# One row block of the third gate chunk ahead of each query and each key-value chunk, and probabilities times values one step later

## The chip, the cores and the metric

The kernel runs on one core of a Trainium2 chip. The metric is the time of one execution in microseconds (us) on the device; for a kernel the median of several runs is given. Profiles come from one execution that the hardware profiler recorded. Five engines matter: TensorE (PE; its weight loads are shown as PEld), VectorE (DVE), ScalarE (ACT), GpSimd (POOL) and SyncE (SP), whose queue issues the weight transfers.

## What is computed

The reference is one encoder layer on 256 tokens of width 4096, in float32. Cut to what matters here:

```
h = rms_norm(x, g_mix);  proj = h @ w_in
c_q, c_kv, k_rope, gate_a, q_b, k_b, v_b, gate_b = split(proj)   # 1024, 512, 64, then 5 x 2048
q  = rms_norm(c_q)  @ w_uq      # 16 heads x (128 + 64 rotary)
kv = rms_norm(c_kv) @ w_ukv     # 16 heads x (128 key + 128 value)
y_a = softmax(q k^T) v          # 16 latent heads, each 256 x 256 scores
y_a = rms_norm(y_a) * silu(gate_a)
y_b = dilated attention of q_b, k_b, v_b, normalised, * silu(gate_b)
x = x + concat(y_a, y_b) @ w_out
x = x + (p @ w_ple) * sigmoid(rms_norm(x) @ w_ple_gate)
out = rms_norm(x)
```

## The kernel before

Every float32 product is done as three products of rounded parts: an operand is split in a high part (ScalarE copies it with rounding, L115) and a low part (VectorE subtracts, L116), and `mm` (L130) issues high x high (L133), then L134 and L135 with one low part each. In the trace the names of the outputs tell them apart: `m` are chunk products, `s` scores, `o` probabilities times values, `t` transposes.

The weights pass through TensorE in *steps*, which are laid out by hand in one list. A `Chunk` is a column block of a weight matrix, and one of its steps takes `per` row blocks of 128 rows (two where nothing else is said): a transfer by SyncE into a `raw` tile (four of them), the split into `hi` and `lo` (a ring of three), and products for both token tiles of 128 tokens. In the main loop (L1425), at each step `i`, first the split of step `i + 2` is queued on ScalarE and VectorE, then the products of step `i` on TensorE, and then `advance()` (L240) moves all running tasks by one stage. Each engine's program order is the order in which this Python code issues.

Tasks are generators; each `yield` ends a stage. `advance()` first starts at most one waiting head (not sooner than two steps behind the last one started, and at most five at a time), then moves the `urgent` tasks, then the running heads, the oldest first.

The stage of the latent heads has eight rounds. Round `i` has a step of the third gate chunk `ga2` (512 columns of the gate, 32 row blocks, two a step, in banks m0 and m1), four steps of query chunk `i` (384 columns, 8 row blocks) and two steps of key-value chunk `i` (512 columns, 4 row blocks). The last two share banks m2 and m3. Behind the last query step `done_uq` (L472) begins: ScalarE copies the product to a tile `T5` (L478), GpSimd rotates the rotary part (L212 to L215), ScalarE copies again (L483), TensorE transposes (L488), and ScalarE and VectorE store the result (L492, L493). Behind the last key-value step `done_uk` (L498) takes the keys (L511, VectorE) and the split values (L118, ScalarE; L119, VectorE) out of the banks, one token tile after the other, and puts two heads in the waiting list, which may start once `done_uq` has ended. The first one of such a pair is called head A, the second head B.

A latent head is the generator `attend` (L386) with `dil` false. Its stages, one for each step: transposes of query and key (L393, L394); their split; scores `s` (ten products); maximum and exponentials (L415, L417); reciprocal and scaling (L433, L438); transposes of the probabilities (L443); their split into `pt` (L446); probabilities times values `o` (six products); the copy of `o` to the head's output and its square (L456, L458). Transposes take the banks t0 and t1 in turn; there is one bank each for `s` and `o`.

After the eight rounds the remaining eight steps of `ga2` and sixteen of a fourth gate chunk `ga3` follow, while the last heads end. Then come the projections of the dilated heads, those heads themselves with the last gate chunks, the output projection and the last stage with the embeddings.

Of the kernel before, what the change touches and what calls it, by code (L numbers as in the profile page):

```python
# [66 lines left out]
class Chunk:  # L67
# [1 line left out]

    def __init__(self, src, nk, n, lhs, banks, done, needs=lambda j: (), per=2, ts=(0, 1), keep=None):
        self.src, self.nk, self.n, self.lhs, self.banks = src, nk, n, lhs, banks
        self.done, self.needs, self.per, self.ts, self.keep = done, needs, per, ts, keep
        self.ps = None


@with_exitstack
def encoder_layer(ctx: ExitStack, tc: tile.TileContext, x, p, positions, g_mix, w_in, g_q_latent, w_uq,
# [18 lines left out]
    def bank(tag, shape, bufs=1):  # L98
        names[tag] = names.get(tag, 0) + 1
        return pp.tile([P, *shape], F32, tag=tag, name=f"{tag}_{names[tag]}", bufs=bufs)  # L100
# [8 lines left out]
    def plain(t):  # L109
        return t.bitcast(F32)  # L110

    def split(hi, lo, src, scale=None):

        if scale is None:
            nc.scalar.activation(hi, src, AF.Copy)  # L115
            nc.vector.tensor_tensor(lo, src, plain(hi), op=ALU.subtract)  # L116
        else:
            nc.scalar.activation(hi, src, AF.Copy, scale=scale)  # L118
            nc.vector.scalar_tensor_tensor(lo, src, scale, plain(hi), op0=ALU.mult, op1=ALU.subtract)  # L119
# [266 lines left out]
    def attend(h, q_src, k_src, pe, v, y, dil):  # L386

        tp = turn_bank([4, P])
        for t in range(NT):
            nc.tensor.transpose(tp[:, t], q_src(t), ident)  # L393
            nc.tensor.transpose(tp[:, NT + t], k_src(t), ident)  # L394
        yield
        qk = slot(f"T{h % 2}", [2, 4 * P], F32R)
        split(qk[:, 0], qk[:, 1], tp.rearrange("p a b -> p (a b)"))
        if dil:
            flags.add(("read", h))
        yield  # L400
        s = bank("s", [NT, S])
        for t in range(NT):
            a = tuple(qk[:, i, t * P:(t + 1) * P] for i in range(2))
            b = tuple(qk[:, i, S:] for i in range(2))
            mm(s[:, t], a, b, True, pe is None)
            if pe is not None:
                both = pe[0]()[:, t * P:(t + 1) * P]
                nc.tensor.matmul(s[:, t], both, pe[1][0], start=False, stop=False)
                nc.tensor.matmul(s[:, t], both, pe[1][1], start=False, stop=True)
        yield  # L410
        i = h % 2
        e = E["t"][:, i]
        nmax, l, rl = E["s"][:, i, 0], E["s"][:, i, 1], E["s"][:, i, 2]
        if not dil:
            nc.vector.tensor_reduce(nmax, s, axis=AX.X, op=ALU.max, negate=True)  # L415
            for t in range(NT):
                nc.scalar.activation(e[:, t], s[:, t], AF.Exp, bias=nmax[:, t:t + 1], accum_out=l[:, t:t + 1])  # L417
        else:
            flat = "p a b -> p (a b)"
            nc.vector.scalar_tensor_tensor(e.rearrange(flat), E["d"][:, 0].rearrange(flat), -SLOPES[h],  # L420
                                           s.rearrange(flat), op0=ALU.mult, op1=ALU.add)
            nc.vector.tensor_reduce(nmax, e, axis=AX.X, op=ALU.max, negate=True)
            yield
            for t in range(NT):
                nc.scalar.activation(e[:, t], e[:, t], AF.Exp, bias=nmax[:, t:t + 1])
            yield
            for t in range(NT):
                nc.vector.scalar_tensor_tensor(e[:, t], e[:, t], 1.0, E["d"][:, 1, t], op0=ALU.mult,
                                               op1=ALU.mult, accum_out=l[:, t:t + 1])
            nc.vector.reciprocal(rl, l)  # L430
        yield
        if not dil:
            nc.vector.reciprocal(rl, l)  # L433
        for t in range(NT):
            if dil:
                nc.scalar.activation(e[:, t], e[:, t], AF.Copy, scale=rl[:, t:t + 1])
            else:
                nc.vector.tensor_scalar(e[:, t], e[:, t], rl[:, t:t + 1], None, op0=ALU.mult)  # L438
        yield
        tp = turn_bank([NT, S])  # L440
        for k in range(NT):
            for t in range(NT):
                nc.tensor.transpose(tp[:, k, t * P:(t + 1) * P], e[:, t, k * P:(k + 1) * P], ident)  # L443
        yield
        pt = slot(f"T{2 + h % 2}", [2, NT, S], F32R)
        split(pt[:, 0], pt[:, 1], tp)  # L446
        if dil:
            vs = slot(("Q0", "T6")[h % 2], [2, NT, HD], F32R)
            split(vs[:, 0], vs[:, 1], v)
            v = lambda kt: (vs[:, 0, kt], vs[:, 1, kt])  # L450
        yield
        o = bank("o", [S])
        for k in range(NT):
            mm(o, v(k), tuple(pt[:, i, k] for i in range(2)), k == 0, k == NT - 1)
        yield
        nc.scalar.activation(y, by_token(o) if dil else o, AF.Copy)  # L456
        sq = junk[:, S * i:S * (i + 1)] if h else acc
        nc.scalar.activation(sq, o, AF.Square)  # L458
        if h:
            nc.gpsimd.tensor_tensor(acc, acc, sq, op=ALU.add)  # L460
        flags.add(("head", dil, h))

    def by_token(a):
        return a.rearrange("p (t c) -> p t c", t=NT)
# [7 lines left out]
    def done_uq(i):  # L472
        def task(ps):
            q = slot("T5", [NT, 2, NOPE + ROPE])
            kq = slot("T6", [1024])
            pairs[i] = {"q": q, "kq": kq}
            for t in range(NT):
                nc.scalar.activation(q[:, t].rearrange("p h c -> p (h c)"), ps[t], AF.Copy, scale=rqs[:, t:t + 1])  # L478
            both = kq[:, 512:].rearrange("p (t h d r) -> p t h d r", t=NT, h=2, d=2)
            rotate(both[:, :, :, 0], q[:, :, :, NOPE:], both[:, :, :, 1], 2)  # L480
            yield
            yield
            nc.scalar.activation(both[:, :, :, 1], both[:, :, :, 0], AF.Copy)  # L483
            yield
            tp = turn_bank([2, S])
            for h in range(2):
                for t in range(NT):
                    nc.tensor.transpose(tp[:, h, t * P:(t + 1) * P], both[:, t, h].rearrange("p d r -> p (d r)"),  # L488
                                        ident)
            yield  # L490
            pe = slot("Q0", [2, S], F32R)
            nc.scalar.activation(pe, tp, AF.Copy)  # L492
            nc.vector.tensor_tensor(pe[ROPE:], tp[ROPE:], plain(pe[ROPE:]), op=ALU.subtract)  # L493
            pairs[i]["pe"] = pe
            flags.add(("uq", i))
        return task
# [28 lines left out]
    def lhs_c(key):  # L525
        return lambda kt: (cT[key][0][:, kt], cT[key][1][:, kt])
# [227 lines left out]
    class Step:  # L754
# [4 lines left out]
        def __init__(self, load, split, run, needs=(), frees=0):  # L759
            self.load, self.split, self.run, self.needs, self.frees, self.after = load, split, run, needs, frees, None  # L760
            self.ring = WP
# [363 lines left out]
    M = ("m0", "m1"), ("m2", "m3")  # L1125
# [8 lines left out]
    def add(ch, lo=0, hi=None):  # L1134
        steps.extend((ch, j) for j in range(lo, ch.nk // ch.per if hi is None else hi))

    def cols(w, lo, n):
        return w[:, lo:lo + n]
# [59 lines left out]
    lay(blk, order, gates_mid(blk), gates_done(blk))  # L1198
    ga2 = from_x(OFF_GA + 1024, 512, done_gate(0, 2))
    ga2.banks, other = M  # L1200
    for i in range(8):
        add(ga2, i, i + 1)
        add(Chunk(cols(w_uq, 384 * i, 384), 8, 384, lhs_c("q"), other, done_uq(i), lambda j: ["latents"]))
        add(Chunk(cols(w_ukv, 512 * i, 512), 4, 512, lhs_c("kv"), other, done_uk(i), lambda j: ["latents"]))
    hook(len(steps), lambda: spawn(y_stats(0)))
    hook(len(steps) + 1, lambda: spawn(x_sums()))
# [21 lines left out]
    for c in range(4):  # L1228
        if c == 3:
            hook(len(steps) + 8, lambda: spawn(y_sums()))  # L1230
        ch = from_x(OFF_GB + 512 * c, 512, done_gate(1, c))
# [33 lines left out]
    for c, (lo, n) in enumerate(blocks):  # L1265
        if c < 2 * WIDE:
            continue
        w, per = cols(w_ple_gate, lo, n), 1024 // n
# [20 lines left out]
    class Old(Step):  # L1289
# [40 lines left out]

        def run(self, hi, lo):
            ch, j = self.ch, self.j
            if j == 0:
                ch.ps = [bank(b, [512]) for b in ch.banks]
            for k in range(ch.per):
                kt = ch.per * j + k
                a = ch.lhs(kt)
                for t in ch.ts:
                    mm(ch.ps[t][:, :ch.n], tuple(q[:, t * P:(t + 1) * P] for q in a), (hi[:, k], lo[:, k]),
                       kt == 0, kt == ch.nk - 1)  # L1340
            if ch.per * (j + 1) == ch.nk:
                self.after = lambda: ch.done([q[:, :ch.n] for q in ch.ps])
# [82 lines left out]
    for i, step in enumerate(steps):  # L1425
# [23 lines left out]
        n = 0  # L1449
# [33 lines left out]
```

## Time and profile before

| | |
|---|---|
| median of 3 runs | 1947.0 us (1946.75 to 1947.37) |
| the profiled execution | 1946.98 us, span 1944.7 us |
| mean granted TensorE clock | 0.997 |
| busy share of the span | PE 99%, PEld 84%, DVE 76%, ACT 55%, POOL 4% |
| bytes moved by DMA | 370.57 MB, mean 191 GB/s |
| share of the chain that ended last | PE 96%, DVE 2%, ACT 1% |

The profile's span begins with the first recorded instruction; the execution's own time is 2.3 us longer. Times in the trace are us from the span's start. The latent stage with its eight rounds runs from about 243 us to 433 us. In the timeline a row has the start, the duration, the engine, the line, the operation, output and input names and shapes, and the count; what stands in brackets is how long the engine was idle before it and what it waited for. The durations of products are modelled and overlap, so distances between starts are the better measure. A row of the waits has who waited for whom, the us in total, the times and the longest.

### The profile page before, as it was taken

The page shows a single profiled execution, that of the slowest core. Times are in us where ns is not written, and L with a number is a line of the kernel's source. Part 1 is how long each engine was busy: PE and PEld are TensorE (multiplying, and loading weights), DVE is VectorE, ACT ScalarE, POOL GpSimd, SP SyncE. Part 2 cuts the span into 40 slices and gives each one's busy share as a digit, 9 for nine tenths or more (in the row PEclk, how much of TensorE's full clock was granted, in tenths as well). Part 3 has the DMA queues.
Part 4 walks back from the last instruction along what each step waited for, and adds up shares of the span by engine and source line. Part 5 has one row for each costly group of instructions (what it writes and reads, how often), then busy time and mean ns, then how long its engine had stood idle before and what let it go on. Part 6 is the DMA issues. An engine that isn't in the chain of part 4 may idle for free.

```text
span 1944.7 us, 25491 instructions
## 1 busy us (share of the span) xinstructions
PE 1918.8 (99%) x9317; PEld 1636.6 (84%) x9317; DVE 1487.4 (76%) x2053; ACT 1079.2 (55%) x1478; POOL 81.6 (4%) x124
## 2 busy tenths in 40 slices
PE   9999999999999999999999999999999999999997
PEld 8998888888888888888888888888888888888887
DVE  7767965556888878878677777888866598888765
ACT  6555565555555555545446676555555455655543
POOL 1001012221000000000000100000000000000000
PEclk9999999999999999999999999999999999999999
DMA  7666654445566666566664446665656556566655
GB/s 249 189 184 197 195 168 127 125 138 163 180 209 205 200 201 217 191 199 196 202 210 141 152 143 225 211 213 183 206 188 218 187 189 218 191 222 203 225 185 178
DMA packets 146476, 370.57 MB, mean 191 GB/s; under 512 B 11924, under 2 KB 45808, under 8 KB 146096
## 3 DMA queue, kind: packets, MB, share of 16 engines
q1 hardware_dynamic: 144432, 361.80, 58.2%
q0 software_dynamic: 1920, 7.15, 1.1%
q8 instruction: 73, 1.20, 0.2%
q14 instruction: 51, 0.42, 0.1%
HBM read 364.72 MB, written 4.19 MB: 190 GB/s over the span
## 4 chain that ended last, share of the span: by engine, by line
PE 96%; DVE 2%; ACT 1%; DMA 0%; issue 0%; SPq 0%; DVEq 0%; ACTq 0%
PE m L133 20%; PE m L134 20%; PE m L135 20%; PE t L133 4%; PE t L135 4%; PE t L134 4%; PE o L134 4%; PE o L135 4%; PE o L133 4%; PE s L133 3%; PE s L135 3%; PE s L134 3%; PE t L443 1%; DVE lo L116 1%; ACT hi L115 0%; DMA raw<-in_w_in_dram 0%
## 5 line engine op out<-in xcount | busy, mean ns | idle before, releaser
L116 DVE TENSOR_TENSOR lo<-raw,hi 128x1024 fp32r<-128x1024 f32 (+4 forms) x495 | 552.4, 1127 | 255.9 <-ACT hi L115 254.7
L115 ACT ACTIVATE hi<-raw 128x1024 fp32r<-128x1024 f32 (+4 forms) x495 | 482.4, 982 | 330.0 <-PE m L135 138.4
L133 PE MATMUL m<-hi,Ah 128*128 128x512 f32 (+2 forms) x1118 | 423.8, 379 | 0.0
L134 PE MATMUL m<-lo,Ah 128*128 128x512 f32 (+2 forms) x1118 | 419.0, 375 | 0.7 <-DVE lo L832 0.5
L135 PE MATMUL m<-hi,Al 128*128 128x512 f32 (+2 forms) x1114 | 416.7, 374 | 0.0
L134 PEld LDWEIGHTS m<-lo,Ah 128*128 128x128 f32 x1118 | 210.8, 189 | 31.5 <-DVE lo L116 1.2
L135 PEld LDWEIGHTS m<-hi,Al 128*128 128x128 f32 x1114 | 209.8, 188 | 32.5 <-DVE Al L127 0.2
L133 PEld LDWEIGHTS m<-hi,Ah 128*128 128x128 f32 x1118 | 210.8, 189 | 29.6
L133 PE MATMUL m<-hi,B 128*128 128x512 f32 (+1 forms) x405 | 154.2, 381 | 4.1 <-ACT T L478 3.9
L135 PE MATMUL m<-hi,B 128*128 128x512 f32 (+1 forms) x405 | 150.7, 372 | 0.0
L134 PE MATMUL m<-lo,B 128*128 128x512 f32 (+1 forms) x405 | 150.7, 372 | 0.0
L116 DVE TENSOR_TENSOR B<-raw,B 128x1024 fp32r<-128x1024 f32 (+1 forms) x81 | 87.1, 1088 | 27.7 <-ACT B L115 27.7
L115 ACT ACTIVATE B<-raw 128x1024 fp32r<-128x1024 f32 (+1 forms) x81 | 75.8, 950 | 53.7 <-PE o L135 25.8
L133 PEld LDWEIGHTS m<-hi,B 128*128 128x128 f32 x405 | 76.1, 188 | 16.1 <-ACT T L478 6.1
L135 PEld LDWEIGHTS m<-hi,B 128*128 128x128 f32 x405 | 76.0, 188 | 11.2
L134 PEld LDWEIGHTS m<-lo,B 128*128 128x128 f32 x405 | 76.2, 188 | 10.3 <-DVE lo L116 0.2
L829 ACT ACTIVATE hi<-raw 128x1024 fp32r<-128x1024 f32 x50 | 53.2, 1065 | 54.7 <-PE o L135 22.5
L115 ACT ACTIVATE hi<-B 128x1024 fp32r<-128x1024 f32 x44 | 46.7, 1061 | 41.3 <-PE o L135 28.5
L116 DVE TENSOR_TENSOR T<-t,T 128x512 fp32r<-128x512 f32 (+1 forms) x65 | 43.8, 683 | 32.7 <-ACT T L115 32.5
L133 PE MATMUL m<-B,Ah 128*128 128x512 f32 (+1 forms) x184 | 68.5, 372 | 0.0
L135 PE MATMUL m<-B,Al 128*128 128x512 f32 (+1 forms) x184 | 68.2, 371 | 0.0
L134 PE MATMUL m<-B,Ah 128*128 128x512 f32 (+1 forms) x184 | 68.2, 371 | 0.0
(744 smaller groups left out, 3778.9 us busy)
## 6 DMA issues: line engine op xcount, KB each, us to landing
raw<-in_w_in_dram SPq DMA_DIRECT2D x320, 512.0 KB, 3.9
raw<-in_w_out_dram SPq DMA_DIRECT2D x128, 512.0 KB, 4.6
raw<-in_w_ple_gate_dram SPq DMA_DIRECT2D x128, 512.0 KB, 4.5
raw<-in_w_in_dram SPq DMA_DIRECT2D x63, 400.0 KB, 3.3
raw<-in_w_uq_dram SPq DMA_DIRECT2D x32, 384.0 KB, 3.3
raw<-in_w_ukv_dram SPq DMA_DIRECT2D x16, 512.0 KB, 3.5
T<-in_x_dram SPq DMA_DIRECT2D x7, 512.0 KB, 6.3
T<-in_x_dram POOLq DMA_DIRECT2D x7, 512.0 KB, 7.4
```

Source lines behind the costliest of these rows:

```text
L115: nc.scalar.activation(hi, src, AF.Copy)
L116: nc.vector.tensor_tensor(lo, src, plain(hi), op=ALU.subtract)
L133: nc.tensor.matmul(ps, ah, bh, start=start, stop=False)
L134: nc.tensor.matmul(ps, ah, bl, start=False, stop=False)
L135: nc.tensor.matmul(ps, al, bh, start=False, stop=stop)
L443: nc.tensor.transpose(tp[:, k, t * P:(t + 1) * P], e[:, t, k * P:(k + 1) * P], ident)
L829: nc.scalar.activation(hi, r[1], AF.Copy)
```

## The change

`ga2_1` is a second chunk over the same columns with one row block a step; it stands ahead of each query chunk and of each key-value chunk. The eight steps of two row blocks in the rounds become sixteen of one; the row blocks that are done by the end of the rounds are the same sixteen. The banks are allotted at the first step of `ga2_1` and handed on to `ga2` (`rest`), which does the other sixteen row blocks as before. In `attend`, a latent head has one more `yield` between the split of the probabilities and `o`.

```
-    def __init__(..., per=2, ts=(0, 1), keep=None):
+    def __init__(..., per=2, ts=(0, 1), keep=None, rest=None):
...
-        self.ps = None
+        self.ps, self.rest = None, rest
...
         pt = slot(f"T{2 + h % 2}", [2, NT, S], F32R)
         split(pt[:, 0], pt[:, 1], tp)
+        if not dil:
+            yield
...
     ga2.banks, other = M
+    ga2_1 = Chunk(ga2.src, 32, 512, lhs_x, M[0], None, per=1, rest=ga2)
     for i in range(8):
-        add(ga2, i, i + 1)
+        add(ga2_1, 2 * i, 2 * i + 1)
         add(Chunk(cols(w_uq, 384 * i, 384), 8, 384, lhs_c("q"), other, done_uq(i), lambda j: ["latents"]))
+        add(ga2_1, 2 * i + 1, 2 * i + 2)
         add(Chunk(cols(w_ukv, 512 * i, 512), 4, 512, lhs_c("kv"), other, done_uk(i), lambda j: ["latents"]))
...
         def run(self, hi, lo):
             ch, j = self.ch, self.j
-            if j == 0:
+            if ch.ps is None:
                 ch.ps = [bank(b, [512]) for b in ch.banks]
+                if ch.rest:
+                    ch.rest.ps = ch.ps
```

More of the change, by code (lines that the diff above doesn't have):

```diff
@@ L67, with __init__ @@
 class Chunk:
-    def __init__(self, src, nk, n, lhs, banks, done, needs=lambda j: (), per=2, ts=(0, 1), keep=None):
+    def __init__(self, src, nk, n, lhs, banks, done, needs=lambda j: (), per=2, ts=(0, 1), keep=None, rest=None):
         self.src, self.nk, self.n, self.lhs, self.banks = src, nk, n, lhs, banks
         self.done, self.needs, self.per, self.ts, self.keep = done, needs, per, ts, keep
-        self.ps = None
+        self.ps, self.rest = None, rest
 @with_exitstack
```

## The prediction

> **What bounds the kernel now.** I read the page first, then TensorE's waits, then the timeline of the stage that the diff edits.
>
> ```profile
> PE 1918.8 (99%) x9317; PEld 1636.6 (84%) x9317; DVE 1487.4 (76%) x2053; ACT 1079.2 (55%) x1478; POOL 81.6 (4%) x124
> ```
> ```profile
> PE o L134 <- DVE T L116: 5.5, 7, 0.9
> PE m L133 <- ACT T L478: 3.9, 7, 0.6
> PE t L270 <- DVE lo L116: 1.6, 1, 1.6
> PE m L1416 <- DVE junk L1410: 1.5, 1, 1.5
> PE t L443 <- DVE T L438: 0.3, 1, 0.3
> ```
>
> TensorE is busy all the time, and nothing in the diff changes the number of its products. So only its waits can be won or lost. Outside the start and end the list (us in total, times, longest) has two that repeat, both in the latent stage: the output product `o` waiting for the low half of the probabilities, and the first key-value product waiting for L478, which copies the query chunk out of its bank. A round of that stage takes 24.65 us:
>
> ```profile
> 294.65:319.30 24.65, 23.23 (x138) 21.13 (x137) 14.85 (x24) 13.91 (x30) 6.01 (x9) 1.00 0.42 128
> ```
>
> I call the steps of a round G (two row blocks of the third gate chunk), U0 to U3 (query chunk) and K0, K1 (key-value chunk); heads A and B are the pair whose latents the previous round made. The timeline of TensorE in a round (start, duration):
>
> ```profile
> 288.96 0.28 PE L133 MATMUL o<-T,B 128*128 128x256 f32 x1
> 290.08 0.39 PE L134 MATMUL o<-T,B 128*128 128x256 f32 x1 [0.85 <-DVE T L116]
> ...
> 298.08 0.27 PE L394 MATMUL t<-ident,T 128*128 128x128 f32 x1
> 298.91 0.50 PE L133 MATMUL m<-hi,B 128*128 128x512 f32 x1 [0.56 <-ACT T L478]
> 299.25 0.39 PE L134 MATMUL m<-lo,B 128*128 128x512 f32 x1
> ...
> 304.49 0.28 PE L133 MATMUL s<-T 128*128 128x256 f32 x1
> ...
> 305.68 0.40 PE L133 MATMUL m<-hi,Ah 128*128 128x512 f32 x1
> ...
> 308.44 0.60 PE L488 MATMUL t<-ident,T 128*128 128x128 f32 x4
> 308.87 0.29 PE L443 MATMUL t<-ident,T 128*128 128x128 f32 x1
> ```
>
> From these I take: G's 12 products last 308.44-305.68 = 2.76 us, 0.23 each, so a half G is 1.38; ten score products `s` last 305.68-304.49 = 1.19, 0.12 each; four transposes 0.43, 0.11 each. The first gap is 290.08-288.96-0.12 = 1.00. The second is 298.91-298.08-0.11 = 0.72. After a wait the next product also starts late: 299.25-298.91 = 0.34 instead of 0.23, so 0.11 more. The two waits cost 1.11 and 0.83 us in a full round.
>
> **What the change takes away.** With half a G (g') between U3 and K0, the copy L478 has 1.38 us of products beside it, and head B's transposes no longer stand between U3 and K0 (L478 waits for them now, because they read the tile it overwrites). Taking 0.83 in seven rounds, and 0.43 in the first (rows below: 254.37-254.05 = 0.32, and 0.11), gives 6.2. `o` with another step between loses its wait: six times 1.11, and a seventh idle of 5.5-6x0.85 = 0.4, with the same 0.26 on top 0.66, gives 7.3. With the 0.3 of L443 the gain is 13.8 us at most.
>
> **What it adds.** I wrote down which stage of which head falls behind which step. A round becomes g, U0 to U3, g', K0, K1. The query task finishes one step earlier, so head A starts behind U0 and B behind U2, each with ten stages. Behind the steps TensorE then does: g: B's probability transposes (L443); U0: `o` of A; U2: `o` of B, `s` of the next A, transposes of the next B; g': `s` of the next B; K0: L443 of A; K1: L488. Two places have only half a G of cover, and each comes behind a chain that can begin only when the step before it ends.
>
> *Scores of B, behind g'.* ScalarE works in program order. Behind U3 it has the two L478 copies, the two copies of the last B's output, A's two exponentials, then the high half of B's query-key split; VectorE follows with the low half. How soon L478 comes after U3 shows best in the first round:
>
> ```profile
> 253.36 0.33 PE L135 MATMUL m<-hi,B 128*128 128x384 f32 x1
> ...
> 253.88 0.34 PE L135 MATMUL m<-hi,B 128*128 128x384 f32 x1
> 254.37 0.50 PE L133 MATMUL m<-hi,B 128*128 128x512 f32 x1
> ```
> ```profile
> 253.74 1.11 ACT L478 ACTIVATE T<-m,st 128x384 f32<-128x384 f32 x2 [0.66 <-PE m L135]
> 254.74 1.05 ACT L115 ACTIVATE hi<-raw 128x1024 fp32r<-128x1024 f32 x1
> ...
> 290.98 0.38 ACT L456 ACTIVATE B<-o 128x256 f32<-128x256 f32 x1 [0.72 <-PE o L135]
> ...
> 291.53 1.10 ACT L115 ACTIVATE T<-t 128x512 fp32r<-128x512 f32 x2
> ...
> 302.17 0.48 ACT L417 ACTIVATE T<-s,st 128x256 f32<-128x256 f32 x1 [1.34 <-DVE st L415]
> ...
> 303.09 0.60 ACT L115 ACTIVATE T<-t 128x512 fp32r<-128x512 f32 x1
> ```
> ```profile
> 303.72 0.69 DVE L116 TENSOR_TENSOR T<-t,T 128x512 fp32r<-128x512 f32 x1 [1.58 <-ACT T L115]
> ```
>
> U3's last product starts at 253.88; three products earlier is 253.36, so each takes 0.17 and U3 ends at 254.05. L478 begins 0.05 after the first token tile is done (253.36+0.33), and ScalarE is free at 254.74, 0.69 after U3. The two output copies take 291.53-290.98 = 0.55, the exponentials 303.09-302.17 = 0.92, from high half to low half is 0.63, the low half 0.69, the signal 0.05: 3.53 us after U3. TensorE gets there after g' and one product that needs only the high half: 1.38+0.12 = 1.50. The wait is 2.03, with the restart 2.14; the first such round has no output copies, 1.59. Seven rounds: 6x2.14+1.59 = 14.4 us.
>
> *Probability transposes of B, behind the next g.* Behind K1, VectorE and ScalarE unload the key-value chunk (L511, L118, L119 for each token tile), then split A's probabilities, then VectorE scales B's probabilities, which L443 transposes.
>
> ```profile
> 259.47 0.48 DVE L511 TENSOR_SCALAR T<-m,st 128x256 f32<-128x256 f32 x1 [0.20 <-PE m L135]
> ...
> 289.34 0.69 DVE L116 TENSOR_TENSOR T<-t,T 128x512 fp32r<-128x512 f32 x1
> 289.94 0.16 DVE L433 RECIPROCAL st<-st 128x2 f32<-128x2 f32 x1
> ...
> 305.33 0.48 DVE L511 TENSOR_SCALAR T<-m,st 128x256 f32<-128x256 f32 x1
> ...
> 308.17 0.15 DVE L433 RECIPROCAL st<-st 128x2 f32<-128x2 f32 x1
> 308.36 0.61 DVE L438 TENSOR_SCALAR T<-T,st 128x256 f32<-128x256 f32 x2
> ```
> ```profile
> 259.94 0.39 PE L133 MATMUL m<-hi,Ah 128*128 128x512 f32 x1
> ```
> ```profile
> 307.63 0.83 ACT L115 ACTIVATE hi<-raw 128x768 fp32r<-128x768 f32 x1
> ```
>
> L511 can start 0.47 before K1 is through (259.47 against 259.94). From it to ScalarE's next work is 307.63-305.33 = 2.30, to the low half of A's split 0.63 more, 2.93; VectorE itself is free at 308.17-305.33 = 2.84, so 2.93 holds. The low half takes 289.94-289.34 = 0.60, the reciprocal 0.19, and L443 followed the scaling's start by 308.87-308.36 = 0.51: 4.23, or 3.76 after K1's end. TensorE arrives after L488 and half a G: 0.43+1.38 = 1.81. Now it arrives after the scores, a whole G and L488, 1.19+2.76+0.43 = 4.38, and there is no split before the scaling: that is why L443 waits only 0.3 in all. The new wait is 1.95; six rounds 11.7, and in the last, where a whole G follows, 3.76-0.43-2.76 = 0.57. Together 12.3 us. While L443 waits, U0's bank comes free (VectorE has gone on 2.84 us after L511), so it costs nothing more.
>
> *Small things.* Two more changes a round between transposes and products cost between nothing and the 0.11 of a restart each, 0 to 1.5 us in seven rounds; I take 1.2, near the upper end, since a late product is what every switch in these rows shows. The gate block's split becomes two of 128x512 (0.60 and 0.69 against 1.05 for the large one on ScalarE): about 0.15 us more on each engine, twice a round, under TensorE's products. `o` one step later and one step earlier a start finish the last head behind the same step, so the following stages keep their place. Eight more transfers pass SP's queue:
>
> ```profile
> SPq L1306 <- DVE lo L116: 591.9, 239, 7.9
> ```
>
> SP waits for buffers to be emptied, not the splits for data, so smaller transfers cost nothing; if every one of eight were late by its landing time, that would be the third rival. [...]
>
> The sum: 14.4+12.3+1.2-13.8 = +14.1 us. The profiled execution took 1946.98 us (span 1944.7), the median of the runs is 1947.0. So 1961.0 us.
>
> **Rivals.** *Both covers hold* (faster): if what I queue behind L478 and L511 were done before them, the gains stay and the two new waits do not come: 1947.0-13.8 = 1933.2. Against it: ScalarE sat idle 0.66 before L478 in the row above with work behind it. Chance 0.08. *One of the two new waits does not come*: only the first, 14.4+1.2-13.8 = +1.8; only the second, -0.3. Both are no change that a measurement tells. Chance 0.04. *Transfers late*: the half blocks land 3.9 us after issue as the large ones do, 8x3.9 = +31 over the forecast, 1992:
>
> ```profile
> raw<-in_w_in_dram SPq DMA_DIRECT2D x320, 512.0 KB, 3.9
> ```
>
> Chance 0.02. *Clock*: the granted clock is 1.00 in the round quoted, with gaps of 1 us. If gaps of 2 us lowered it to half for as long as one G, each of 13 waits would cost 2.76 more, 36 us, 1997. Chance 0.02, since no gap reaches it. [...] My forecast has the remaining 0.84.
>
> **How the numbers follow.** Low bound of the forecast: no cost for switching (-1.2), and A's split not ahead of the scaling (-0.6 six times): 1956; some more overlap that I missed, three us, 1953. High: if L478 and L511 could not start on the first token tile while the second is computed, the chains are some 0.5 us longer in 7 places and 0.7 in 6: +7.7, 1969. The range is 1953 to 1970. A measurement of this kernel tells about 0.2%, 3.9 us, from no change; slower takes the forecast, the transfers and the clock, 0.88; same 0.04; faster 0.08.
>
> **What would show it.** In the changed profile the waits of K0 on L478 and of `o` on L116 are gone; instead `s` waits for T (L115, L116) about seven times by 2 us in all its pieces, and L443 for the scaling (by 2 us, six times); a round takes about 26.7 to 27.3 us. Wrong if a round is under 24.65, if either wait is absent, or if waits stand in the stages behind.

## The result and the profile after

The changed kernel takes 1969.28 us (median of 4 runs, 1968.84 to 1969.7) against 1947.04 us; the ratio is 1.0114, 95% interval 1.0097 to 1.0132. It is 22.2 us slower. The forecast was 14.1 us slower, 1961.0 us, with a range from 1953 to 1970. TensorE's busy line of the page and its granted clock in 40 slices:

```profile
PE 1928.8 (98%) x9317; PEld 1641.3 (83%) x9317; DVE 1491.1 (76%) x2061; ACT 1080.4 (55%) x1486; POOL 68.4 (3%) x124
PEclk9999999899999999999999999999999999999999
```

TensorE has the same 9317 products, but it is busy for 1928.8 us instead of 1918.8: some of them became slower. One slice, in the latent stage, has a clock of 8 tenths. TensorE's three longest waits (us in total, times, longest; lines are one to three higher than before, by the lines that the change adds):

```profile
PE t L444 <- DVE T L439: 11.3, 7, 1.8
PE s L134 <- ACT T L116: 8.0, 7, 1.2
PE s L135 <- DVE T L117: 2.4, 7, 0.3
```

The two old waits are gone, and the two forecast ones are there, seven times each. Five rounds of the stage, from one L444 to the next (start and end, length, busy times, granted clock, DMA share, GB/s):

```profile
286.79:315.26 28.47, 25.09 (x136) 22.16 (x137) 15.40 (x26) 14.24 (x31) 3.41 (x8) 0.94 0.35 111
315.26:342.15 26.89, 23.51 (x136) 20.95 (x137) 15.37 (x26) 14.12 (x31) 4.30 (x9) 1.00 0.42 118
342.15:370.60 28.45, 25.07 (x137) 22.32 (x137) 15.38 (x26) 14.24 (x31) 4.29 (x9) 0.94 0.37 111
370.60:400.63 30.03, 26.64 (x137) 23.74 (x137) 15.38 (x26) 14.36 (x31) 4.13 (x9) 0.89 0.38 105
400.63:427.52 26.89, 23.51 (x136) 20.95 (x137) 15.37 (x26) 14.12 (x31) 4.29 (x9) 1.00 0.38 119
```

Where the clock is 1.00, a round takes 26.89 us; the forecast was 24.65 + 2.14 + 1.95 + 0.2 - 1.94 = 27.0. The other rounds are longer by 1.56 to 1.58, or by 3.14, and in these the clock is below 1.00. The timeline of TensorE in the first of them:

```profile
300.38 0.40 PE L136 MATMUL m<-hi,Al 128*128 128x512 f32 x1
302.00 0.39 PE L134 MATMUL s<-T 128*128 128x256 f32 x1 [1.23 <-ACT T L116]
302.73 0.39 PE L135 MATMUL s<-T 128*128 128x256 f32 x1 [0.34 <-DVE T L117]
...
303.42 0.28 PE L135 MATMUL s<-T 128*128 128x256 f32 x1
303.54 0.36 PE L136 MATMUL s<-T 128*128 128x256 f32 x1
...
304.13 0.63 PE L134 MATMUL m<-hi,B 128*128 128x512 f32 x1
304.56 0.63 PE L135 MATMUL m<-lo,B 128*128 128x512 f32 x1
...
306.69 0.55 PE L134 MATMUL m<-hi,B 128*128 128x512 f32 x1
307.08 0.39 PE L135 MATMUL m<-lo,B 128*128 128x512 f32 x1
307.31 0.40 PE L136 MATMUL m<-hi,B 128*128 128x512 f32 x1
...
313.05 0.40 PE L136 MATMUL m<-hi,Al 128*128 128x512 f32 x1
315.26 0.72 PE L444 MATMUL t<-ident,T 128*128 128x128 f32 x4 [1.82 <-DVE T L439]
```

After the half block ends (300.38 + 0.23) TensorE stands still until 302.00 and, but for one product, until 302.73: 2.00 us. Behind that, from 303.6 to 307.0, products start 0.43 us apart instead of 0.23: half clock for 3.4 us (granted clock 0.50). There are five such stretches in this execution, beginning at 303.6, 358.2, 371.9, 388.9 and 443.6, with a granted clock of 0.50 or 0.51 in each. The distances are 54.6, 13.7, 17.1 and 54.6, all whole multiples of 3.41. Five times 1.57 is 7.9 us: with the forecast's 14.1 this is 22.0 of the 22.2 us.

The two chains, on ScalarE and on VectorE, are as forecast:

```profile
298.90 1.10 ACT L481 ACTIVATE T<-m,st 128x384 f32<-128x384 f32 x2 [2.88 <-PE m L136]
299.90 0.38 ACT L459 ACTIVATE B<-o 128x256 f32<-128x256 f32 x1
...
300.43 0.49 ACT L418 ACTIVATE T<-s,st 128x256 f32<-128x256 f32 x1
...
301.32 0.62 ACT L116 ACTIVATE T<-t 128x512 fp32r<-128x512 f32 x1
```
```profile
301.98 0.69 DVE L117 TENSOR_TENSOR T<-t,T 128x512 fp32r<-128x512 f32 x1 [4.09 <-ACT T L116]
...
311.03 0.48 DVE L514 TENSOR_SCALAR T<-m,st 128x256 f32<-128x256 f32 x1 [0.71 <-PE m L136]
...
313.96 0.69 DVE L117 TENSOR_TENSOR T<-t,T 128x512 fp32r<-128x512 f32 x1
...
314.76 0.62 DVE L439 TENSOR_SCALAR T<-T,st 128x256 f32<-128x256 f32 x2
```

ScalarE stood idle 2.88 us before the query chunk's copy (now L481), with the exponentials and the split that TensorE needs queued behind it. VectorE unloads the bank from 311.03, then comes the split (313.96), then the scaling (314.76), and L444 begins 0.50 later.

### The profile page after: what moved, and what is told of

The parts are those of the page before. It is cut to its first block, busy times and chain, and to the rows that moved or that the text cites. A ratio compares the mean times of both kernels' runs of the same rounds, so it can differ in the third digit from the quotient of the medians.

```text
span 1967.1 us, 25558 instructions
## 1 busy us (share of the span) xinstructions
PE 1928.8 (98%) x9317; PEld 1641.3 (83%) x9317; DVE 1491.1 (76%) x2061; ACT 1080.4 (55%) x1486; POOL 68.4 (3%) x124
## 4 chain that ended last, share of the span: by engine, by line
PE 95%; DVE 3%; ACT 1%; issue 0%; DMA 0%; POOL 0%; SPq 0%; DVEq 0%; ACTq 0%; POOLq 0%
PE m L134 20%; PE m L135 20%; PE m L136 20%; PE t L134 4%; PE t L136 4%; PE t L135 4%; PE o L136 4%; PE o L134 4%; PE o L135 4%; PE s L135 3%; PE s L136 3%; PE s L134 3%; PE t L444 1%; DVE T L117 1%; DVE lo L117 0%; DVE B L120 0%
## 5 line engine op out<-in xcount | busy, mean ns | idle before, releaser
L116 ACT ACTIVATE hi<-raw 128x1024 fp32r<-128x1024 f32 (+4 forms) x503 | 480.9, 965 | 360.9 <-PE m L136 160.0
L134 PE MATMUL m<-hi,Ah 128*128 128x512 f32 (+2 forms) x1104 | 418.3, 379 | 0.4 <-ACT Ah L126 0.4
L135 PE MATMUL m<-lo,Ah 128*128 128x512 f32 (+2 forms) x1104 | 413.1, 374 | 0.8 <-DVE lo L835 0.5
L134 PE MATMUL m<-hi,B 128*128 128x512 f32 (+2 forms) x415 | 161.1, 388 | 0.7 <-DVE B L120 0.7
L135 PE MATMUL m<-lo,B 128*128 128x512 f32 (+2 forms) x415 | 156.8, 378 | 0.7 <-DVE lo L117 0.5
L136 PE MATMUL m<-hi,B 128*128 128x512 f32 (+2 forms) x415 | 156.8, 378 | 0.0
L117 DVE TENSOR_TENSOR B<-raw,B 128x1024 fp32r<-128x1024 f32 (+1 forms) x85 | 93.0, 1108 | 27.2 <-ACT B L116 27.0
L116 ACT ACTIVATE B<-raw 128x1024 fp32r<-128x1024 f32 (+1 forms) x85 | 81.0, 966 | 51.3 <-PE o L136 21.7
L134 PEld LDWEIGHTS m<-hi,B 128*128 128x128 f32 x415 | 79.7, 192 | 12.2 <-issue 1.2
L136 PEld LDWEIGHTS m<-hi,B 128*128 128x128 f32 x415 | 79.2, 191 | 12.0
L116 ACT ACTIVATE hi<-B 128x1024 fp32r<-128x1024 f32 x46 | 48.8, 1061 | 47.5 <-PE o L136 30.1
L134 PE MATMUL m<-B,Ah 128*128 128x512 f32 (+1 forms) x196 | 73.3, 374 | 0.0
L136 PE MATMUL m<-B,Al 128*128 128x512 f32 (+1 forms) x196 | 72.9, 372 | 0.0
L135 PE MATMUL m<-B,Ah 128*128 128x512 f32 (+1 forms) x196 | 72.9, 372 | 0.0
L832 ACT ACTIVATE hi<-raw 128x1024 fp32r<-128x1024 f32 x44 | 46.8, 1063 | 41.3 <-PE t L136 22.1
```

The costliest lines, as they stand in the source:

```text
L134: nc.tensor.matmul(ps, ah, bh, start=start, stop=False)
L135: nc.tensor.matmul(ps, ah, bl, start=False, stop=False)
L136: nc.tensor.matmul(ps, al, bh, start=False, stop=stop)
L832: nc.scalar.activation(hi, r[1], AF.Copy)
```

## The experiments

Each kernel is compared with the kernel before on the same chip: 1947.16 us for the two parts alone, the filled gaps and the order that takes both chains away, 1946.05 us for the other four.

**One part alone: the half blocks.** The changed kernel without its second part:

```
         split(pt[:, 0], pt[:, 1], tp)
-        if not dil:
-            yield
```

> The changed kernel without its second part: the gate's half blocks stay, probabilities times values come one step after their split as before. My theory (each new wait is a chain on ScalarE and VectorE that has only half a gate block of products beside it): the scores of head B still wait behind the gate's half block, by about 1.4 us for the high half and the low half together, and now the output product of head A waits about 1 us too, because it comes behind a half block; the probability transposes of head B wait for nothing, they come two steps later. Round about 26.2 us against 24.65 before and 26.9 after; time about 1954 (+7). [...] Rival (the half blocks are the gain, the later output product is the loss): below 1947, by up to 6 us.

Measured: 1953.83 us, ratio 1.0035 (1.0021 to 1.0049), +6.7 us. TensorE's waits:

```profile
PE s L134 <- ACT T L116: 4.8, 7, 0.7
PE o L134 <- ACT T L116: 3.3, 6, 0.5
PE s L135 <- DVE T L117: 2.4, 7, 0.3
PE o L135 <- DVE T L117: 2.1, 6, 0.3
```

The time and the waits are as expected to a few tenths: the scores wait (0.7 and 0.3 idle), and the output product too. The round is not: from one copy of the query chunk to the next it takes 25.63 us, where I gave 26.2, which did not fit my own time of 1954. The half blocks lose by themselves.

**The other part alone: the output product later.** The kernel before with the `yield` added.

> The kernel before with only the second part: the output product of the latent heads one step later, whole gate blocks. My theory: the output product's wait (0.85 idle a round) goes, but heads then stay one step longer, so that the scaling of the next probabilities is queued on VectorE behind a split and the probability transposes wait about 1.2 us; the wait of the first key-value product for the query chunk's copy stays (0.56). Round about 25.2 us, time about 1951 (+4), clock 1.00. Rival (the wait just goes): -7 us, 1940.

Measured: 1956.17 us, ratio 1.0047 (1.0032 to 1.0062), +9.0 us; the wait list has

```profile
PE t L443 <- DVE T L438: 11.7, 14, 1.5
PE m L133 <- ACT T L480: 3.9, 7, 0.6
```

The rival (the wait just goes) fell, and the mechanism stands: the output product's wait became one of the probability transposes. Its size was too low in my expectation: it measured 1.5 us a round and a second one of 0.2, instead of 1.2. So both parts lose alone. Their losses (6.7 and 9.0) sum to 15.7, near the 14.4 that the changed kernel loses without half clock (next experiment), but that is no proof that they add up: the waits are not the same ones. In the changed kernel those at the output product and at L480's copy are gone, the two that remain are longer, and the clock comes on top.

**The clock: the same waits, with TensorE kept at work.** The changed kernel with products that nobody reads in the gaps:

```
+    def fill(n):
+        w, some = bank("o", [512]), ident.bitcast(mybir.dt.bfloat16)
+        for _ in range(n):
+            nc.tensor.matmul(w[:, :256], some[:, :P], some[:, :256], start=True, stop=True)
...
+        if not dil and h % 2 and h < 15:
+            fill(11 if h > 1 else 5)
         s = bank("s", [NT, S])
...
+        if not dil and h % 2 and h < 13:
+            fill(15)
         tp = turn_bank([NT, S])
```

> The changed kernel, with products of a constant tile, whose result nobody reads, put into the two new gaps of TensorE: 11 products of 256 columns ahead of head B's scores, 15 ahead of its probability transposes. No engine other than TensorE does more, and the chains that TensorE waits for are the same. Theory of the clock (a stretch of 3.4 us with about 1.9 us or more of it idle is followed by 3.4 us at half clock; five such stretches in the changed profile): no stretch at half clock is left, every round takes about 26.9 us, time about 1961. Rival (the half clock comes from something else, or is only shown and costs nothing): the time stays at 1969 or grows.

Measured: 1961.59 us (1961.33 to 1962.41), ratio 1.0077 (1.0062 to 1.0092). That is 7.7 us less than the changed kernel, with more work on TensorE. The filling stands where the gaps were, and the clock over 28 us in the middle of the stage is 1.00:

```profile
300.83 1.38 PE L390 MATMUL o<-ident 128*128 128x256 bf16 x11
302.94 0.39 PE L135 MATMUL s<-T 128*128 128x256 f32 x1 [0.34 <-DVE T L117]
...
311.92 1.81 PE L390 MATMUL o<-ident 128*128 128x256 bf16 x15
313.90 0.72 PE L453 MATMUL t<-ident,T 128*128 128x128 f32 x4 [0.17 <-DVE T L446]
```
```profile
343.00:371.00 28.00, 27.48 (x172) 24.44 (x171) 16.44 (x27) 14.51 (x31) 4.30 (x9) 1.00 0.40 121
```

The scores and the transposes begin as long after the half block as in the changed kernel: the chains are the same, only the half clock is gone. From one copy of the query chunk to the next a round now takes 26.90 us each time, as the changed kernel's rounds at full clock do (26.89). So the clock is 7.7 us of the 22.2, and what is left, 14.4 over the kernel before on this chip, is the queues' share. The 1.9 us of the expectation is the author's estimate; the waits ahead of the five stretches are of 1.98 and 2.00 us.

**The clock by itself: nine added gaps.** The kernel before, with nine gaps in the output projection, where TensorE otherwise waits for nothing:

```
+    gaps = {gap_at + 3 + 3 * k: n for k, n in enumerate((2, 3, 4, 5, 6, 7, 6, 5, 4))}
+    def gap(n):
+        w = bank("o", [512])
+        nc.tensor.transpose(w[:, :P], ident, ident)
+        nc.scalar.activation(junk[:, :P], w[:, :P], AF.Copy)
+        for _ in range(n):
+            nc.scalar.activation(junk[:, :P], junk[:, :P], AF.Copy)
+        nc.tensor.transpose(w[:, P:2 * P], junk[:, :P], ident)
...
+            if i in gaps:
+                gap(gaps[i])
```

> The kernel before, with nine gaps of TensorE made on purpose in the last two chunks of the output projection, where it waits for nothing otherwise: behind every third step of 2.7 us a transpose of a constant, a chain of 3 to 8 short ScalarE copies that begins with it, and a transpose that needs the end of the chain. The output is not touched. The gaps should last about 1.2 us (shortest chain) to 2.7 us (longest), each alone in a stretch of 8 us. [...] The time is longer by the nine gaps, about 20 us, plus up to 1.7 us for each half-clock stretch.

A single run: 1976.32 us, 30.3 more than the kernel before, a few us above what I expected. (The 1.7 us for a stretch is an estimate: half of the 3.41 us that one lasts in the changed kernel's trace.) The gaps hold 18.2 us of idle by the brackets, which count from the modelled end of the product in front; counted from where a next product could start, each gap is about 0.16 longer. The ends of four of the gaps (TensorE's timeline; the first two are the third and fourth gap):

```profile
1515.63 0.33 PE L1434 MATMUL o<-ident,junk 128*128 128x128 f32 x1 [1.79 <-ACT junk L1433]
...
1526.43 0.33 PE L1434 MATMUL o<-ident,junk 128*128 128x128 f32 x1 [2.13 <-ACT junk L1433]
...
1565.87 0.33 PE L1434 MATMUL o<-ident,junk 128*128 128x128 f32 x1 [2.47 <-ACT junk L1433]
1576.66 0.33 PE L1434 MATMUL o<-ident,junk 128*128 128x128 f32 x1 [2.13 <-ACT junk L1433]
```

Half clock began at 1526.6, 1540.3, 1553.9 and 1577.8, for 3.4 us each, with a granted clock of 0.50: the distances, 13.7, 13.6 and 23.9, are 4, 4 and 7 times 3.41. By the brackets, it followed the fourth and the eighth gap (2.13 us each), the fifth (2.48) and the sixth (2.81), and none of the five others: 1.11, 1.45, 1.79 (two), and the seventh with 2.47. The seventh was longer than two that half clock followed, so the length of a gap alone does not decide. The four starts give a grid with lines 3.41 us apart and cells between them. One line of it lies at 1564.2, inside this gap (1563.2 to 1565.9), so that no cell of the grid holds more than 1.7 us of it.

**One of the two chains taken away.** The changed kernel, but behind the last key-value step of a round the running heads are moved before the urgent tasks:

```
-        for pool in (urgent, running):
+        for pool in (running, urgent) if heads_first[0] else (urgent, running):
...
+        heads_first[0] = rounds[0] <= i < rounds[1] and (i - rounds[0]) % 8 == 7
```

> The changed kernel, with the running heads ahead of the urgent tasks only behind the last key-value step of a round; behind the query step the order is the changed kernel's. So of the two new waits only the one of the probability transposes is taken away. My theory (two separate chains): the scores of head B wait as in the changed kernel (1.2 us and 0.3 us), the probability transposes do not wait, the next query chunk waits for its bank by up to 1.5 us instead; a round of about 25.5 to 26.5 us; half-clock stretches come behind the scores' wait as in the changed kernel, about four; time about 1957 to 1963. Rival (one chain causes both, so that with one order mended both go): no wait at the scores, 1953 or less.

Measured: 1957.63 us, ratio 1.0056 (1.0041 to 1.0071).

```profile
PE s L134 <- ACT T L116: 8.0, 7, 1.2
PE s L135 <- DVE T L117: 2.4, 7, 0.3
PE m L134 <- DVE B L120: 2.4, 7, 0.7
```

The scores wait exactly as in the changed kernel, the probability transposes no longer, and a smaller wait for the query chunk's bank has come. They are two chains, and the order in the queue makes the second. The scores' wait alone is also enough for half clock: there are four stretches of 3.41 us (from 328.8, 380.0, 407.3 and 434.6), each behind such a wait, as I had expected; the mean granted clock of this execution is 0.993.

**Both chains taken away by order.** The same for all steps of the rounds (`heads_first[0] = rounds[0] <= i < rounds[1]`).

> The changed kernel, but during the eight rounds the running heads are moved ahead of the urgent tasks in each step: head A's exponentials and head B's split stand before the copy L478 on ScalarE, and head A's probability split and head B's scaling before the unloading of the key-value chunk. Nothing else changes, and every half block stays as short. My theory (the order in the queues makes the two waits): both waits go, the query chunk waits about 0.7 us for its bank instead, a round takes 24.2 us or less, time about 1942 (-5 against before), clock 1.00. Rival (half a gate block is too short a cover, whatever the order): waits of 1 to 2 us remain at the scores and the probability transposes, time 1957 to 1970.

Measured: 1953.16 us, ratio 1.0033 (1.0022 to 1.0045).

```profile
PE m L134 <- DVE B L120: 10.4, 13, 1.0
...
PE t L445 <- DVE T L440: 0.2, 1, 0.2
```

Both waits went, as the theory of the order has it, against the rival. But the time I gave, 1942, was wrong: unloading the key-value bank now stands last on VectorE, and the next query chunk waits for its two banks by up to 1.0 us each, 10.4 us in all instead of some 5; two stretches at half clock remain (granted clock 0.50, from 338 and 389). Even a round at full clock takes 24.8 us, more than the 24.65 of the kernel before. The wait was only handed on: with the split, the scaling and the unloading behind half a block, TensorE waited in each order tried.

**The cause of the old wait.** The kernel before, with two tiles in turn for the scaled query chunk; the values of even and odd rounds share another tile for it:

```
+            if i == 0:
+                E["q"] = slot("B1", [2, NT, 2, NOPE + ROPE])
-            q = slot("T5", [NT, 2, NOPE + ROPE])
+            q = E["q"][:, i % 2]
...
+                E["v"] = slot("B0", [2, 2, NT, 2, HD], F32R)
...
-            v = slot(f"B{i % 2}", [2, NT, 2, HD], F32R)
+            v = E["v"][:, i % 2]
```

> The kernel before, steps and stages unchanged, with two tiles for the scaled query chunk in turn instead of one (the space comes from the values of the two rounds, which share another tile). Then the copy L478 need not wait until head B's transposes have read the old tile. My theory of the old wait at the first key-value product (0.56 idle, 0.83 with what goes with it, eight times; the reader of the old tile is the cause, not the lack of products between): the wait goes, the output product still waits; a round of about 23.9 us, time about 1941 (-6). Rival (L478 is simply late after the last query step, and needs products beside it as the change gives): the wait stays, 1947.

Measured: 1931.88 us (1931.49 to 1932.5), ratio 0.9927 (0.9912 to 0.9942): 14.2 us faster than the kernel before and some 37 faster than the changed one. The three longest of TensorE's waits in the whole execution (three more are of 0.5 us and less):

```profile
PE m L1419 <- DVE junk L1413: 1.5, 1, 1.5
PE t L270 <- DMA T<-in_x_dram: 1.4, 1, 1.4
PE m L134 <- DVE lo L835: 0.5, 1, 0.5
```

I expected 6 us, for the wait at the key-value chunk. Both waits of the stage went. In the kernel before, the copy L478 had waited for head B's transposes seven times:

```profile
ACT T L478 <- PE t L393: 22.1, 7, 3.3
```

Here are the copies on ScalarE (now L480), VectorE's unloading behind them, and the first product behind K1:

```profile
292.77 1.10 ACT L480 ACTIVATE B<-m,st 128x384 f32<-128x384 f32 x2 [0.50 <-PE m L135]
...
315.37 1.10 ACT L480 ACTIVATE B<-m,st 128x384 f32<-128x384 f32 x2 [0.50 <-PE m L135]
```
```profile
300.50 0.48 DVE L514 TENSOR_SCALAR T<-m,st 128x256 f32<-128x256 f32 x1 [0.23 <-PE m L135]
```
```profile
300.91 0.28 PE L133 MATMUL s<-T 128*128 128x256 f32 x1
```

A round is 315.37 - 292.77 = 22.60 us instead of 24.65. The copy waits for the query chunk's own products, and no longer for head B's transposes. With it all that stands behind it on ScalarE comes earlier, and VectorE can unload the bank as soon as the product is there (L514 waits for TensorE), where before it was held up by the splits queued ahead of it. It begins 0.41 us before K1's products are through (300.50 and 300.91); in the kernel before it began 0.84 after (305.33 and 304.49). That is 1.25 us sooner, and the output product had waited 0.85. So by these rows the output product's wait was an offspring of the first; no run holds up the unloading alone. The edit also lays the values of two rounds in one tile, but no wait of TensorE in either list is for the values.

**An order tried on top.** The previous kernel, and behind the first query step of a round the heads before the urgent tasks (`(i - rounds[0]) % 7 == 1`).

> As the previous kernel (kernel before, two tiles for the query chunk), and in each round behind the first query step the heads are moved ahead of the urgent tasks, so that the split of head A's probabilities stands before the store of the rotary part (L492, L493) on ScalarE and VectorE. My theory (the output product's wait of 0.85 is the time by which this store, 0.48 on ScalarE and 0.6 on VectorE, goes ahead of the split): the output product's wait falls to about 0.3, a round of about 23.4 us, time about 1938 (-9), better than both kernels. Rival (the split of the large weight tiles in front holds it up): as the previous kernel.

Measured: 1931.89 us, ratio 0.9927 (0.991 to 0.9943), as the previous kernel. There was no wait of the output product left to mend; this separates neither of the two readings of it.

## Why the prediction was right, and where it was not

- *What goes.* Both old waits went, as forecast. The 13.8 us given for them is near the 14.2 that the second query tile won.
- *The scores behind g'.* Forecast 2.03 us of wait with both halves; the timeline has 2.00 (300.61 to 302.73 less one product). Right.
- *The probability transposes behind g.* Forecast 1.95; the timeline has 313.05 + 0.23 to 315.26, 1.98. Right; with the order turned the wait went while the other stayed.
- *The small things.* Transfers, more instructions, more switches: a round without half clock is 26.89 where 27.0 was forecast. No wait of TensorE for the half blocks' transfers is in the list; they landed 2.7 us after issue (median of 16), not the 3.9 that the rival took.
- *The clock.* This step failed. I gave 0.02 to it, "since no gap reaches it"; no run shows a length that a gap has to reach, and in the runs half clock followed waits of 2.00 us and did not follow one gap of 2.47. Its price, too, was wrong in the other direction: I took every one of 13 waits to bring 2.76 us, and five brought 1.57 each. With the filled gaps 1961.59 us was measured: the forecast of 1961.0 is the time of the changed kernel without its half-clock stretches.
- *The range.* That 1969.28 lies inside it is luck. Its upper end was set for two chains that are 0.5 and 0.7 us longer, and they came out as forecast; the 7.7 us of the clock, which the range did not hold, happened to fit in that room.

The trace before already had such a stretch. Near its start TensorE was idle for 1.63 us, and 3.4 us at half clock followed (the second row has a stretch of time with its length, the busy times, the granted clock of 0.50, DMA share and GB/s):

```profile
7.49 1.00 PE L270 MATMUL t<-ident,T 128*128 128x128 f32 x4 [1.63 <-DVE lo L116]
```
```profile
7.59:11.01 3.42, 3.42 (x13) 3.39 (x14) 0.00 (x0) 0.31 (x1) 0.00 (x0) 0.50 1.00 328
```

The wait itself is in the list that the prediction shows (`PE t L270 <- DVE lo L116: 1.6, 1, 1.6`). So gaps of about 2 us in the forecast were a reason to give the clock more than 0.02.

What the rows show of the clock is this. The stretches of half clock last 3.41 us and begin at whole multiples of it from each other: in the changed kernel the first and the last of five lie 140.0 us apart (41 times), in the one with gaps the first and the last of four 51.2 (15 times). The starts so give a grid in each execution, and in the changed kernel each stretch follows a cell of it with 1.98 or 2.00 us of waiting.

That tells apart which waits were hit in the changed kernel. The six full waits of the scores are alike, 2.00 us: four lie whole in one cell and were followed by half clock, and the two others (from 329.1 and 414.4) have a line of the grid in them and were not. Of the six of 1.98 us at the probability transposes one lies whole in a cell, and it alone was followed.

The nearest cases (from where a next product could start): no half clock behind 1.95 us in one cell (third gap, 1513.68 to 1515.63); half clock behind 1.98 with four transposes after it (368.62 to 370.60), behind 2.00 in two pieces (300.61 to 302.73), and in the kernel with both orders turned behind 1.94 in two pieces (from 334.61, where the cell begins, to 337.14). At the start of the kernel before half clock followed 1.63 us by the bracket, with three products and some transposes in the 3.42 us ahead of it (1.70 of these idle in all). So idle time alone does not draw the line; what else counts stays open.

What the forecast did not see at all is that the two old waits had one cause: the copy L478 waited for the transposes that read the tile it overwrites. I had named this reader in the prediction, but took the two waits for separate gains.

## What to carry to other kernels

Before moving work into a wait, ask what the waiting instruction itself waits for: here one more tile for the query chunk removed both waits of a round, while a shorter step in front of one and a later reader for the other only uncovered two other chains. ScalarE stood idle here for 2.88 us before one copy, with other work queued behind it. In a queue that runs in order like this, the cover of a chain is the work between the step that releases it and its reader, so halving a step takes cover from every chain that is counted in steps and has that step in between. Give the clock a price when a forecast has waits of TensorE of some 2 us: five of twelve such waits were followed by half clock here, and each of the five brought 1.57 us. And look for half clock in the trace you already have, its start included.

## What the runs showed that was not expected

- Half clock followed an idle stretch of 1.4 us, one product and 0.6 us more (2.00 us in one cell of 3.41); it did not follow a gap of 2.47 us with a line of the grid in it.
- The stretches differ from round to round with unchanged waits (none, one or two in 26.89, 28.45 and 30.03 us): 26.89 us is 7.88 times 3.41, so the same wait lies elsewhere on the grid in the next round.
- Filling gaps with 26 useless products a round made the changed kernel 7.7 us faster.
